# Input projection of a hybrid encoder block: stores issued by ScalarE, modulation sums as float32r halves, transposes of k some steps later

## Chip, cores and metric

The kernel runs on one core of one Trainium2 chip. The metric is the device time of one execution in microseconds (us). Before the change it is 2694.75 us, the median of 3 runs (2694.58 to 2695.16).

## What is computed

One encoder layer over 2048 tokens of width 1024, all in float32 (D = 1024, 8 query heads and 2 key/value heads of 64, pooling width 512, feed-forward width 2816):

```python
mod = silu(c) @ w_ada + b_ada                     # 6 sections of 1024: sh1, sc1, g1, sh2, sc2, g2
h = rmsnorm(x, norm1_g) * (1 + sc1) + sh1
proj = h @ w_in                                   # [q 512 | k 128 | v 128 | pool 512]
q = apply_axial_rope(rmsnorm(q, q_norm_g)); k = apply_axial_rope(rmsnorm(k, k_norm_g))
att = blocked_gqa(q, k, v)                        # softmax over all 2048 keys
pool = pool_mixer(u_pool, w_pool, pool_scale)     # windows 2, 4, 8, 16
x = x + g1 * (concat(att, pool) @ w_out)
h2 = rmsnorm(x, norm2_g) * (1 + sc2) + sh2
x = x + g2 * conv_gated_ffn(h2, w_up, conv_w, conv_b, w_down)
```

## The kernel before

The whole layer is one program in three stages: the input projection (here up to about 380 us), attention with the output projection, and the feed-forward part. The tile framework sets the semaphores and plans the order of each engine's instructions by its own estimate of when they are ready; some instructions are pinned to the order in which they are written. Each engine takes its queue strictly in order, and a transfer waits in the queue of the engine that issues it until its data are there. SP issues nearly all transfers.

Precision is kept by splitting each float32 operand into a part rounded to float32r (`hi`) and the rest (`lo`), and by three float32r matmuls (hi x hi, hi x lo, lo x hi) for one product. A matmul on float32 data that are not split is one of true float32; the trace shows it as more than one instruction.

**Start.** The modulation sections 1 and 0 are needed first. `gen_acc` (L184) loads the eight 128x1024 tiles of a section of w_ada and VectorE adds them up, each scaled by its entries of silu(c), into `acc` (128 partitions x 1024); what is left is a sum over the partitions. `mod_col` (L205) does it with eight float32 matmuls of one column against ones and gives the section as a column per chunk of 128. The small vectors (b_ada, norms, conv weights) come as rows (L142 to L150), are transposed by TensorE and copied to `cols`. w_in is loaded and split in ten pieces (L321).

**Loop over eight blocks of 256 tokens** (L577). Its TensorE work is `gen_u` (pooling channels, 96 matmul steps) and twice `gen_qkv` (24 steps of two matmuls each); after every step the loop advances generators of other work, each at a rate of its own:

- `nxt` is `gen_h` (L268): load x, its mean of squares on ScalarE, scaling, transposes (L290), modulation, split;
- `ropes` is `gen_rope` (L410): norms of q and k and the rotary positions, on VectorE, POOL and ScalarE, a step every 9 (in the last block 4 in the slow stretch);
- `tr_g` is `gen_tr` (L449): transposes of k (`trk`, L456) and q (`tr`, L470), copied to `kst` and `qst` and stored to k_scr and q_scr; a step every 4 (2 in the slow stretch);
- `mix` is `gen_mix` (L514): windows of the pooling mixer on VectorE, its matmuls `pm` (L535), the results `mst`, stored to mix_scr; a step every 4 (2 in the slow stretch);
- `late` (L569), a step every 8: `gen_row(2)`, `gen_col(3)`, `gen_col(4)`, `gen_row(5)`, the other four modulation sections. `gen_row` sums over the partitions with a 128x128 of ones, so that each partition has the whole row, and adds b_ada by a second matmul of one partition (L242, L243, true float32). After section 2 it scales w_out by the gate, splits it, and stores both parts to wo_scr (L262, L263).

In the last block the order is q, k, v first and then the pooling channels, and `early` (L552) computes some of the maxima of attention's first unit.

**To attention.** k, v and q go through device memory (k_scr, v_scr, q_scr). The last 256 keys are loaded by POOL (L653) once their stores have landed; the matmuls `pmx` (L692) of the first unit need them. SP then loads the split w_out (`wo`, L651), the pooling results (`mix`, L810) and x (L839).

Of the kernel before, what the change touches and what calls it, by code (L numbers as in the profile page):

```python
# [14 lines left out]
ALU = mybir.AluOpType  # L15
# [49 lines left out]
def hybrid_block(ctx: ExitStack, tc: tile.TileContext, x, c, w_ada, b_ada, norm1_g, w_in,  # L65
# [12 lines left out]
    def rows(v):  # L78
        return v.rearrange("(a p) -> a p", p=P)
# [45 lines left out]
    with tc.tile_pool(name="p1", bufs=1) as p1, \  # L125
# [16 lines left out]
        SP.dma_start(out=rows_a[8:56], in_=rows(b_ada))  # L142
        SP.dma_start(out=rows_a[56:64], in_=rows(norm1_g))
        SP.dma_start(out=rows_a[64:72], in_=rows(norm2_g))
        SP.dma_start(out=rows_a[72:76], in_=rows(pool_scale))
        SP.dma_start(out=rows_a[76:120], in_=rows(conv_b))
        cw = conv_w.rearrange("w (a p) -> (w a) p", p=P)
        SP.dma_start(out=rows_a[120:124], in_=cw[128:132])
        rows_b = p1.tile([P, P], F32, tag="rows", name="rows_b", bufs=2)
        SP.dma_start(out=rows_b, in_=cw[0:128])  # L150
# [5 lines left out]
        g10 = p1.tile([P, 10, HD], F32, name="g10")  # L156
        qkrow = p1.tile([P, P], F32, tag="rows", name="qkrow", bufs=2)[0:1, :]
        SP.dma_start(out=qkrow[:, 0:64], in_=q_norm_g.unsqueeze(0))
        SP.dma_start(out=qkrow[:, 64:128], in_=k_norm_g.unsqueeze(0))
        gq = ps1.tile([P, 512], F32, tag="tp", name="gq", bufs=2)  # L160
        PE.matmul(gq[:, 0:128], ones[0:1, :], qkrow, start=True, stop=True)
        for h in range(10):
            V.tensor_copy(out=g10[:, h], in_=gq[:, 0:64] if h < 8 else gq[:, 64:128])
# [40 lines left out]

        def mod_col(sec, slot, acc):  # L205
            ps = ps1.tile([P, 512], F32, tag="pu", name=f"mc{sec}", bufs=2)
            for j in range(KD):
                PE.matmul(ps[:, j:j + 1], acc[:, j * P:(j + 1) * P], ones[:, 0:1], start=True, stop=True)
            tc.keep_in_program_order(
                V.tensor_tensor(out=mod_c[:, slot], in0=ps[:, 0:KD],  # L210
                                in1=cols[:, CB + 8 * sec:CB + 8 * sec + 8], op=ALU.add))
# [11 lines left out]
        def gen_col(sec, slot, cn=None):  # L223
            acc = new_acc(sec)
            yield from gen_acc(sec, acc, stage, eng=BG)
            for _ in range(4):
                yield
            mod_col(sec, slot, acc)
            if cn is not None:
                mod_scale(slot, cn)  # L230
            yield

        def gen_row(sec, slot):
            acc = new_acc(sec)
            yield from gen_acc(sec, acc, stage, eng=BG)
            brow = stage()
            SP.dma_start(out=brow[0:1], in_=b_ada[sec * D:(sec + 1) * D].unsqueeze(0))
            for _ in range(4):
                yield
            for n in range(2):  # L240
                ps = ps1.tile([P, 512], F32, tag="pu", name=f"mr{sec}_{n}", bufs=2)
                PE.matmul(ps, ones, acc[:, n * 512:(n + 1) * 512], start=True, stop=False)  # L242
                PE.matmul(ps, ones[0:1, :], brow[0:1, n * 512:(n + 1) * 512], start=False, stop=True)  # L243
                V.tensor_copy(out=acc[:, n * 512:(n + 1) * 512], in_=ps)
                yield
            if slot == 1:
                SP.dma_start(out=g_scr, in_=acc)
                return
            wss = {}
            ks = (4, 5, 6, 7, 0, 1, 2, 3)  # L250
            for i, k in enumerate(ks):
                for k_ in ks[i:i + 2]:
                    if k_ not in wss:
                        wss[k_] = stage()
                        SP.dma_start(out=wss[k_], in_=w_out[k_ * P:(k_ + 1) * P])
                yield
                ws = wss[k]
                BG.tensor_tensor(out=ws, in0=ws, in1=acc, op=ALU.mult)
                wh = p1.tile([P, D], F32R, tag="woh", name=f"woh{k}", bufs=1)
                S.copy(out=wh, in_=ws)  # L260
                BG.tensor_tensor(out=ws, in0=ws, in1=wh.bitcast(F32), op=ALU.subtract)
                SP.dma_start(out=wo_scr[0, k * P:(k + 1) * P], in_=wh.bitcast(F32))  # L262
                SP.dma_start(out=wo_scr[1, k * P:(k + 1) * P], in_=ws)  # L263
                yield

# [115 lines left out]
        def gen_qkv(b, t, chains):  # L381
# [23 lines left out]
            SP.dma_start(out=v_scr[tok:tok + P], in_=vst.bitcast(F32))  # L405
            cs_t = p1.tile([P, 2, HD], F32, tag="rope", name=f"rope{tok}", bufs=2)
            SP.dma_start(out=cs_t, in_=rope[tok:tok + P])
            chains.append((b, tok, raw, cs_t))

        def gen_rope(b, tok, raw, cs_t, res):  # L410
# [3 lines left out]
            V.tensor_tensor(out=raw, in0=raw, in1=g10, op=ALU.mult)  # L414
# [34 lines left out]
        def gen_tr(tok, qhl, khl):  # L449

            for _ in range(4):
                yield
# [9 lines left out]
            SP.dma_start(out=k_scr[:, :, :, tok:tok + P].rearrange("i a p t -> p (i a) t"), in_=kst)  # L462
# [11 lines left out]
            SP.dma_start(out=q_scr[:, :, tok:tok + P].rearrange("h p t -> p h t"), in_=qst)  # L474
# [39 lines left out]
        def gen_mix(b, us):  # L514
# [10 lines left out]
            for i, g in enumerate(groups(b)):  # L525
# [5 lines left out]
                for _ in range(3):  # L531
                    yield
# [8 lines left out]
            i0 = 8 if b == 0 else 0  # L541
            for i in range(2):
                SP.dma_start(out=mix_scr[i, :, :, t0 - 8 + i0:t0 - 8 + nout].rearrange("g p t -> p g t"),
                             in_=mst[i][:, :, i0:nout].bitcast(F32))
# [890 lines left out]
```

## Time and profile before

| | |
|---|---|
| median of 3 runs | 2694.75 us |
| profiled execution, its own time | 2694.41 us |
| span of the profile | 2692.6 us |
| granted clock of TensorE, mean | 0.988 of full speed |
| TensorE, busy share of the span | 96% |
| VectorE, POOL, ScalarE | 72%, 60%, 57% |
| DMA, read and written | 249.42 and 86.63 MB |

How to read the rows further down. Engines are PE (TensorE matmuls), PEld (its weight loads), DVE (VectorE), ACT (ScalarE), POOL (GpSimd) and SP. In a row of stretches stand the start and end in us, the length, and for PE, PEld, DVE, ACT and POOL the busy time with the number of instructions; then the granted clock as a share of full speed (2.4 GHz; 0.50 is 1.2 GHz), the mean busy share of the 16 DMA engines (above 1 where transfers overlap) and the rate in GB/s. A row of waits reads "who waited, at which line, for whom: us in total, times, longest". A row of groups names line, engine, operation, output and inputs, shape and count, then busy time and mean duration in ns, and the idle time of the engine ahead of it with its releaser. Durations of matmuls overlap, since they are pipelined. A row in order of time has the start, the duration and, in brackets, the idle time before and what ended it.

### The profile page before, as it was taken

The page shows a single profiled execution, that of the slowest core. Times are in us where ns is not written, and L with a number is a line of the kernel's source. Part 1 is how long each engine was busy: PE and PEld are TensorE (multiplying, and loading weights), DVE is VectorE, ACT ScalarE, POOL GpSimd, SP SyncE. Part 2 cuts the span into 40 slices and gives each one's busy share as a digit, 9 for nine tenths or more (in the row PEclk, how much of TensorE's full clock was granted, in tenths as well). Part 3 has the DMA queues.
Part 4 walks back from the last instruction along what each step waited for, and adds up shares of the span by engine and source line. Part 5 has one row for each costly group of instructions (what it writes and reads, how often), then busy time and mean ns, then how long its engine had stood idle before and what let it go on. Part 6 is the DMA issues. An engine that isn't in the chain of part 4 may idle for free.

```text
span 2692.6 us, 38997 instructions
## 1 busy us (share of the span) xinstructions
PE 2577.8 (96%) x13439; PEld 2232.5 (83%) x13439; DVE 1926.2 (72%) x3014; ACT 1544.4 (57%) x2848; POOL 1615.7 (60%) x1397
## 2 busy tenths in 40 slices
PE   5899989999999999989899999899999999999999
PEld 5788877777776776767898999699999998999998
DVE  7877678889999999888577776745555557455554
ACT  5565457767778777776654555554343445544442
POOL 1222135656566666664887887586565676777673
PEclk9999989999999999999999999999999999999999
DMA  9685373431222122223544444533332325333332
GB/s 293 233 266 180 100 242 103 149 100 58 71 63 77 58 76 69 78 88 120 172 149 135 148 132 139 195 106 103 105 106 94 95 78 189 114 122 118 110 110 86
DMA packets 318161, 338.61 MB, mean 126 GB/s; under 512 B 24656, under 2 KB 226330, under 8 KB 317962
## 3 DMA queue, kind: packets, MB, share of 16 engines
q1 hardware_dynamic: 316953, 332.31, 39.1%
q0 software_dynamic: 1008, 3.81, 0.5%
q8 instruction: 105, 1.72, 0.3%
q14 instruction: 95, 0.77, 0.1%
HBM read 249.42 MB, written 86.63 MB: 125 GB/s over the span
## 4 chain that ended last, share of the span: by engine, by line
PE 47%; DVE 2%; POOL 1%; ACT 1%; issue 1%; DMA 0%; DVEq 0%; SPq 0%; POOLq 0%; ACTq 0%
PE py L1248 16%; PE px L1159 13%; PE pw L1159 9%; PE pz L1159 8%; PE pl L1377 1%; DVE b L993 0%; POOL wl_s L1035 0%; ACT hb L977 0%; POOL t L1000 0%; DVE y L1253 0%; DMA wr<-in_w_up_dram 0%; POOL t L1007 0%; POOL wl_a L1035 0%; ACT ac L1218 0%; DVE t L993 0%
## 5 line engine op out<-in xcount | busy, mean ns | idle before, releaser
L741 POOL TENSOR_TENSOR acc<-acc,ph 128x512 f32<-128x512 f32 x352 | 463.6, 1317 | 40.7 <-ACT ph L735 15.5
L1035 POOL TENSOR_TENSOR wl_s<-s,wh_s 128x512 fp32r<-128x512 f32 x260 | 349.6, 1346 | 204.7 <-ACT wh_s L1033 202.1
L735 ACT ACTIVATE ph<-S 128x512 fp32r<-128x512 f32 x512 | 306.9, 600 | 130.0 <-PE S L732 114.3
L737 DVE TENSOR_TENSOR pl<-S,ph 128x512 fp32r<-128x512 f32 x512 | 348.0, 683 | 40.0 <-ACT S L736 33.0
L1253 DVE TENSOR_TENSOR y<-py,y 128x512 f32<-128x512 f32 x300 | 205.8, 688 | 222.4 <-PE py L1248 220.7
L694 DVE TENSOR_REDUCE mx<-pmx 128x1 f32<-128x512 f32 x500 | 337.4, 680 | 25.9 <-PE pmx L692 23.9
L1033 ACT CAST wh_s<-s 128x512 fp32r<-128x512 f32 x264 | 163.5, 621 | 313.0 <-PE pw L1159 146.8
L1035 POOL TENSOR_TENSOR wl_a<-wr,wh_a 128x512 fp32r<-128x512 f32 x195 | 266.7, 1374 | 104.7 <-ACT wh_a L1033 104.3
L736 ACT ACTIVATE S<-S 128x512 f32<-128x512 f32 x512 | 306.5, 599 | 0.0
L1248 PE MATMUL py<-wdh,gh 128*128 128x512 f32 x664 | 261.7, 395 | 1.9 <-DVE y L1253 1.7
L1248 PE MATMUL py<-wdh,gl 128*128 128x512 f32 x664 | 262.1, 395 | 0.0
L1248 PE MATMUL py<-wdl,gh 128*128 128x512 f32 x664 | 261.8, 395 | 0.0
L1033 ACT CAST wh_a<-wr 128x512 fp32r<-128x512 f32 x198 | 122.3, 618 | 240.8 <-PE pz L1159 202.4
L1159 PE MATMUL px<-t,wh_s 128*128 128x322 f32 (+1 forms) x1024 | 247.9, 322 | 5.3 <-ACT p1s L1192 3.6
L724 PE MATMUL B<-pl,vt 128*128 128x512 f32 x512 | 210.5, 411 | 5.3 <-DVE pl L737 5.0
L723 PE MATMUL A<-ph,vt 128*128 128x512 f32 x512 | 204.6, 408 | 5.3 <-ACT ph L735 5.3
L692 PE MATMUL pmx<-kA,qa 128*128 128x512 f32 x500 | 203.2, 408 | 3.4 <-DMA kA<-k_scr 2.5
L732 PE MATMUL S<-qb,kB 65*128 65x512 f32 x512 | 202.8, 402 | 1.1 <-ACT qb L702 0.8
L731 PE MATMUL S<-qa,kA 128*128 128x512 f32 x512 | 202.4, 398 | 0.0
L739 POOL TENSOR_TENSOR acc<-ph,ph 128x512 f32<-128x512 f32 x32 | 41.3, 1290 | 255.4 <-ACT ph L735 234.9
L1159 PEld LDWEIGHTS px<-t,wh_s 128*128 128x128 f32 x1024 | 178.3, 189 | 12.3 <-ACT p1s L1192 4.4
L1159 PE MATMUL px<-t,wl_s 128*128 128x322 f32 (+1 forms) x512 | 164.2, 321 | 0.0
(297 smaller groups left out, 6877.9 us busy)
## 6 DMA issues: line engine op xcount, KB each, us to landing
wr<-in_w_up_dram SPq DMA_DIRECT2D x132, 512.0 KB
wdh<-wd_scr SPq DMA_DIRECT2D x88, 256.0 KB
wdl<-wd_scr SPq DMA_DIRECT2D x88, 256.0 KB
stage<-in_w_ada_dram SPq DMA_DIRECT2D x36, 512.0 KB
x_scr<-x SPq DMA_DIRECT2D x48, 256.0 KB
wds<-in_w_down_dram SPq DMA_DIRECT2D x44, 256.0 KB
wd_scr<-wdh SPq DMA_DIRECT2D x44, 256.0 KB
wd_scr<-wdl SPq DMA_DIRECT2D x44, 256.0 KB
```

The lines of the kernel that those rows point to most:

```text
L694: V.tensor_reduce(out=mx[:, qt, j:j + 1], in_=ps, axis=AX.X, op=ALU.max)
L723: PE.matmul(A, vt[:, kt, 192 * a:192 * a + P], ph, start=kt == 0, stop=kt == NKT - 1)
L724: PE.matmul(B, vt[:, kt, 64 + 64 * a:192 + 64 * a], pl, start=kt == 0, stop=False)
L735: S.activation(out=ph, in_=s, func=AF.Exp, scale=0.125)
L736: S.activation(out=s, in_=s, func=AF.Exp, scale=0.125)
L737: V.tensor_tensor(out=pl, in0=s, in1=ph.bitcast(F32), op=ALU.subtract)
L741: G.tensor_tensor(out=acc, in0=acc, in1=ph.bitcast(F32), op=ALU.add)
L1033: S.copy(out=hf, in_=src)
L1035: eng.tensor_tensor(out=lf, in0=src, in1=hf.bitcast(F32), op=ALU.subtract)
L1159: mm = PE.matmul(ps, l_[:, k], r_[:, k, 0:N], start=first and k == 0 and m == 0, stop=k == 3 and m == 2, skip_group_check=not first)
L1248: PE.matmul(ps, l_[:, ts_], r_, start=i == 0, stop=i == 3 * len(js) - 1)
L1253: V.tensor_tensor(out=ys[t][:, ns], in0=ps, in1=ys[t][:, ns], op=ALU.add)
```

## The change

- The nine small loads ahead of the modulation (rows_a, rows_b, qkrow) are issued by POOL in place of SP.
- The weights of the q and k norms are kept once each (`g2`) and broadcast over the heads; the product is two instructions (8 heads, 2 heads) in place of one.
- For the four late sections the accumulated sum is split into two float32r tiles (`halves`: a copy on ScalarE, a subtraction on VectorE), and the sums over partitions are float32r matmuls of both halves; `gen_row` adds b_ada on one partition before the split. Two more turns of `late` stand before the split (in `gen_row` one more behind the bias). The halves take the two buffers of the tag `stage`.
- The stores of v, k, q, the pooling results and w_out are issued by ScalarE. The store of v moves into the first step of `gen_rope`, those of w_out and of the pooling results come one step after their producers. The rotary tables get 4 buffers in place of 2.
- `gen_tr` waits 7 steps in place of 4 before its first transpose, `gen_mix` 5 in place of 3 before a group's matmuls.

```diff
--- before.py
+++ after.py
@@ -139,28 +139,29 @@
...
         G.memset(rows_a, 0.0)
-        SP.dma_start(out=rows_a[8:56], in_=rows(b_ada))
...
+        G.dma_start(out=rows_a[8:56], in_=rows(b_ada))
...
         cw = conv_w.rearrange("w (a p) -> (w a) p", p=P)
-        SP.dma_start(out=rows_a[120:124], in_=cw[128:132])
+        G.dma_start(out=rows_a[120:124], in_=cw[128:132])
         rows_b = p1.tile([P, P], F32, tag="rows", name="rows_b", bufs=2)
-        SP.dma_start(out=rows_b, in_=cw[0:128])
+        G.dma_start(out=rows_b, in_=cw[0:128])
         tp = ps1.tile([P, 512], F32, tag="tp", name="tpc", bufs=2)
...
-        g10 = p1.tile([P, 10, HD], F32, name="g10")
+        g2 = p1.tile([P, 2, HD], F32, name="g2")
+        ones_r = p1.tile([P, P], F32R, name="ones_r")
+        V.tensor_copy(out=ones_r, in_=ones)
         qkrow = p1.tile([P, P], F32, tag="rows", name="qkrow", bufs=2)[0:1, :]
-        SP.dma_start(out=qkrow[:, 0:64], in_=q_norm_g.unsqueeze(0))
-        SP.dma_start(out=qkrow[:, 64:128], in_=k_norm_g.unsqueeze(0))
+        G.dma_start(out=qkrow[:, 0:64], in_=q_norm_g.unsqueeze(0))
+        G.dma_start(out=qkrow[:, 64:128], in_=k_norm_g.unsqueeze(0))
         gq = ps1.tile([P, 512], F32, tag="tp", name="gq", bufs=2)
         PE.matmul(gq[:, 0:128], ones[0:1, :], qkrow, start=True, stop=True)
-        for h in range(10):
-            V.tensor_copy(out=g10[:, h], in_=gq[:, 0:64] if h < 8 else gq[:, 64:128])
+        V.tensor_copy(out=g2.rearrange("p a d -> p (a d)"), in_=gq[:, 0:128])
@@ -202,12 +203,26 @@
...
+        def halves(sec, acc):
+            hl = [p1.tile([P, D], F32R, tag="stage", name=f"acc{i}_{sec}", bufs=2) for i in range(2)]
+            S.copy(out=hl[0], in_=acc)
+            V.tensor_tensor(out=hl[1], in0=acc, in1=hl[0].bitcast(F32), op=ALU.subtract)
+            return hl
+
         def mod_col(sec, slot, acc):
             ps = ps1.tile([P, 512], F32, tag="pu", name=f"mc{sec}", bufs=2)
-            for j in range(KD):
-                PE.matmul(ps[:, j:j + 1], acc[:, j * P:(j + 1) * P], ones[:, 0:1], start=True, stop=True)
+            if isinstance(acc, list):
+                for j in range(KD):
+                    for i, a_ in enumerate(acc):
+                        PE.matmul(ps[:, 2 * j:2 * j + 2], a_[:, j * P:(j + 1) * P], ones_r[:, 0:2],
+                                  start=i == 0, stop=i == 1)
+                sums = ps[:, 0:2 * KD].rearrange("p (k i) -> p k i", i=2)[:, :, 0]
+            else:
+                for j in range(KD):
+                    PE.matmul(ps[:, j:j + 1], acc[:, j * P:(j + 1) * P], ones[:, 0:1], start=True, stop=True)
+                sums = ps[:, 0:KD]
             tc.keep_in_program_order(
-                V.tensor_tensor(out=mod_c[:, slot], in0=ps[:, 0:KD],
+                V.tensor_tensor(out=mod_c[:, slot], in0=sums,
                                 in1=cols[:, CB + 8 * sec:CB + 8 * sec + 8], op=ALU.add))
@@ -223,9 +238,12 @@
...
             yield from gen_acc(sec, acc, stage, eng=BG)
+            for _ in range(2):
+                yield
+            hl = halves(sec, acc)
             for _ in range(4):
                 yield
-            mod_col(sec, slot, acc)
+            mod_col(sec, slot, hl)
             if cn is not None:
@@ -235,12 +253,17 @@
...
             SP.dma_start(out=brow[0:1], in_=b_ada[sec * D:(sec + 1) * D].unsqueeze(0))
+            for _ in range(2):
+                yield
+            V.tensor_tensor(out=acc[0:1], in0=acc[0:1], in1=brow[0:1], op=ALU.add)
+            yield
+            hl = halves(sec, acc)
             for _ in range(4):
...
                 ps = ps1.tile([P, 512], F32, tag="pu", name=f"mr{sec}_{n}", bufs=2)
-                PE.matmul(ps, ones, acc[:, n * 512:(n + 1) * 512], start=True, stop=False)
-                PE.matmul(ps, ones[0:1, :], brow[0:1, n * 512:(n + 1) * 512], start=False, stop=True)
+                for i, a_ in enumerate(hl):
+                    PE.matmul(ps, ones_r, a_[:, n * 512:(n + 1) * 512], start=i == 0, stop=i == 1)
                 V.tensor_copy(out=acc[:, n * 512:(n + 1) * 512], in_=ps)
@@ -259,9 +282,9 @@
...
                 BG.tensor_tensor(out=ws, in0=ws, in1=wh.bitcast(F32), op=ALU.subtract)
-                SP.dma_start(out=wo_scr[0, k * P:(k + 1) * P], in_=wh.bitcast(F32))
-                SP.dma_start(out=wo_scr[1, k * P:(k + 1) * P], in_=ws)
-                yield
+                yield
+                S.dma_start(out=wo_scr[0, k * P:(k + 1) * P], in_=wh.bitcast(F32))
+                S.dma_start(out=wo_scr[1, k * P:(k + 1) * P], in_=ws)
@@ -402,16 +425,18 @@
...
                                 op=ALU.subtract)
-            SP.dma_start(out=v_scr[tok:tok + P], in_=vst.bitcast(F32))
-            cs_t = p1.tile([P, 2, HD], F32, tag="rope", name=f"rope{tok}", bufs=2)
+            cs_t = p1.tile([P, 2, HD], F32, tag="rope", name=f"rope{tok}", bufs=4)
             SP.dma_start(out=cs_t, in_=rope[tok:tok + P])
-            chains.append((b, tok, raw, cs_t))
-
-        def gen_rope(b, tok, raw, cs_t, res):
+            chains.append((b, tok, raw, cs_t, vst))
+
+        def gen_rope(b, tok, raw, cs_t, vst, res):
             E = V if b >= RB else G
...
             S.activation(out=t1, in_=raw, func=AF.Square)
-            V.tensor_tensor(out=raw, in0=raw, in1=g10, op=ALU.mult)
+            for i, (h0_, h1_) in enumerate(((0, 8), (8, 10))):
+                V.tensor_tensor(out=raw[:, h0_:h1_], in0=raw[:, h0_:h1_],
+                                in1=g2[:, i].unsqueeze(1).broadcast_to([P, h1_ - h0_, HD]), op=ALU.mult)
+            S.dma_start(out=v_scr[tok:tok + P], in_=vst.bitcast(F32))
             yield
@@ -448,7 +473,7 @@
...
-            for _ in range(4):
+            for _ in range(7):
                 yield
@@ -459,7 +484,7 @@
...
             S.copy(out=kst, in_=tr.bitcast(F32))
-            SP.dma_start(out=k_scr[:, :, :, tok:tok + P].rearrange("i a p t -> p (i a) t"), in_=kst)
+            S.dma_start(out=k_scr[:, :, :, tok:tok + P].rearrange("i a p t -> p (i a) t"), in_=kst)
             if tok >= T - BT:
@@ -471,7 +496,7 @@
...
                 S.copy(out=qst[:, hb * 4:hb * 4 + 4], in_=tr.bitcast(F32))
-            SP.dma_start(out=q_scr[:, :, tok:tok + P].rearrange("h p t -> p h t"), in_=qst)
+            S.dma_start(out=q_scr[:, :, tok:tok + P].rearrange("h p t -> p h t"), in_=qst)
@@ -528,7 +553,7 @@
...
                 ph, pl = res[i]
-                for _ in range(3):
+                for _ in range(5):
                     yield
@@ -539,8 +564,9 @@
...
             i0 = 8 if b == 0 else 0
+            yield
             for i in range(2):
-                SP.dma_start(out=mix_scr[i, :, :, t0 - 8 + i0:t0 - 8 + nout].rearrange("g p t -> p g t"),
+                S.dma_start(out=mix_scr[i, :, :, t0 - 8 + i0:t0 - 8 + nout].rearrange("g p t -> p g t"),
                              in_=mst[i][:, :, i0:nout].bitcast(F32))
```

## Rows read from the trace of the kernel before

**Rows 1.** The page, part 1: busy us of each engine over the span.

```profile
PE 2577.8 (96%) x13439; PEld 2232.5 (83%) x13439; DVE 1926.2 (72%) x3014; ACT 1544.4 (57%) x2848; POOL 1615.7 (60%) x1397
```

**Rows 2.** Stretches of time: the engines from PE to POOL, clock, DMA share, GB/s.

```profile
39.00:380.00 341.00, 310.50 (x2006) 284.13 (x2004) 259.22 (x508) 193.79 (x438) 74.59 (x104) 0.96 0.62 197
87.40:90.70 3.30, 3.30 (x18) 3.30 (x17) 3.30 (x5) 0.00 (x0) 0.00 (x0) 0.50 0.46 159
238.40:244.90 6.50, 6.50 (x34) 6.50 (x33) 4.27 (x9) 2.22 (x6) 0.00 (x0) 0.54 0.20 81
375.00:394.50 19.50, 14.64 (x33) 8.42 (x34) 11.54 (x23) 6.21 (x11) 5.46 (x7) 0.50 1.04 371
```

**Rows 3.** TensorE's waits, 45 to 425 us: us in total, times, longest.

```profile
PE mr L242 <- DVE macc L200: 6.4, 2, 4.8
PE trk L456 <- ACT khl L437: 5.6, 3, 3.0
PE tp L290 <- ACT xt L278: 3.8, 3, 1.8
PE pm L535 <- DVE mst L539: 3.2, 2, 2.7
...
PE pm L535 <- ACT ph L508: 2.3, 3, 1.0
```

**Rows 4.** Groups by shape, 45 to 425 us: busy us, mean ns, idle before.

```profile
L242 PE MATMUL mr<-macc,ones 128*128 128x512 f32 x8 | 6.8, 972 | 6.4 <-DVE macc L200 6.4
...
L243 PE MATMUL mr<-stage,ones 1*128 1x512 f32 x8 | 5.2, 759 | 0.0
...
L565 PE MATMUL pme<-k_early,q_early 128*128 128x512 f32 x12 | 5.0, 413 | 0.0
```

**Rows 5.** SP in order of time: start us, us, what.

```profile
70.89 3.12 SPq L190 DMA_DIRECT2D stage<-in_w_ada_dram  x2
```

**Rows 6.** Issues of two stores by SP (ns), waits of SP and ScalarE.

```profile
L405 SPq DMA_DIRECT2D v_scr<-vst x16: 319/330/1831, 74.1 to 355.3; - x16
...
L543 SPq DMA_DIRECT2D mix_scr<-mst x16: 359/408/2697, 109.8 to 379.5; - x16
...
SPq L405 <- DVE vst L403: 20.6, 12, 3.9
...
ACT junk L276 <- DMA xt<-in_x_dram: 13.3, 5, 5.9
```

**Rows 7.** Groups by shape, 45 to 425 us, VectorE and ScalarE.

```profile
L414 DVE TENSOR_TENSOR raw<-raw,g 128x640 f32<-128x640 f32 x16 | 13.1, 819 | 2.2 <-ACT t L413 2.1
...
L444 DVE TENSOR_TENSOR qhl<-raw,qhl 128x512 fp32r<-128x512 f32 x16 | 11.0, 684 | 1.3 <-ACT qhl L443 1.2
...
L261 DVE TENSOR_TENSOR stage<-stage,woh 128x1024 f32<-128x1024 f32 x8 | 9.8, 1219 | 1.7 <-ACT woh L260 1.7
...
L260 ACT CAST woh<-stage 128x1024 fp32r<-128x1024 f32 x8 | 8.4, 1052 | 4.9 <-DVE stage L258 4.9
...
L438 DVE TENSOR_TENSOR khl<-raw,khl 128x128 fp32r<-128x128 f32 x16 | 4.6, 286 | 4.6 <-ACT khl L437 4.6
```

**Rows 8.** The start: two stretches; SP and VectorE in order of time.

```profile
0.00:10.00 10.00, 0.24 (x1) 0.18 (x1) 7.12 (x6) 3.04 (x4) 3.61 (x79) 1.00 0.74 269
10.00:20.00 10.00, 1.89 (x7) 1.26 (x7) 7.25 (x16) 1.01 (x2) 0.00 (x0) 1.00 0.86 294
...
9.11 0.35 SPq L150 DMA_DIRECT2D rows_b<-in_conv_w_dram  x1
...
21.99 0.75 DVE L198 TENSOR_SCALAR macc<-big_h_lo,cact 128x1024 f32<-128x1024 f32 x1 [2.52 <-DMA big_h_lo<-in_w_ada_dram]
```

**Rows 9.** The end of the projection: POOL, SP and TensorE in order of time.

```profile
376.65 0.57 POOL L653 DMA_DIRECT2D kA<-k_scr  x1 [2.90 <-DMA k_scr<-kst]
...
380.02 2.03 SPq L651 DMA_DIRECT2D wo<-wo_scr  x2
...
382.19 1.22 PE L692 MATMUL pmx<-kA,qa 128*128 128x512 f32 x2 [2.46 <-DMA kA<-k_scr]
```

More of the change, by code (lines that the diff above doesn't have):

```diff
@@ L141, in hybrid_block @@
         G.memset(rows_a, 0.0)
-        SP.dma_start(out=rows_a[8:56], in_=rows(b_ada))
[L143 to L146, printed above, removed]
+        G.dma_start(out=rows_a[8:56], in_=rows(b_ada))
+        G.dma_start(out=rows_a[56:64], in_=rows(norm1_g))
+        G.dma_start(out=rows_a[64:72], in_=rows(norm2_g))
+        G.dma_start(out=rows_a[72:76], in_=rows(pool_scale))
+        G.dma_start(out=rows_a[76:120], in_=rows(conv_b))
         cw = conv_w.rearrange("w (a p) -> (w a) p", p=P)
-        SP.dma_start(out=rows_a[120:124], in_=cw[128:132])
+        G.dma_start(out=rows_a[120:124], in_=cw[128:132])
         rows_b = p1.tile([P, P], F32, tag="rows", name="rows_b", bufs=2)
-        SP.dma_start(out=rows_b, in_=cw[0:128])
+        G.dma_start(out=rows_b, in_=cw[0:128])
         tp = ps1.tile([P, 512], F32, tag="tp", name="tpc", bufs=2)
```

## The prediction

> **What bounds the kernel now.** I read the page's busy shares first: TensorE is busy in 96% of the span, no other engine above 72% [rows 1], so time is lost only where TensorE idles, runs at its low clock or does dear work. The change touches the input projection alone, so the table by stretches comes next. From 39 to 380 us TensorE is busy 310.50 of 341.00 us at a mean granted clock of 0.96 [rows 2]: 30.5 us of idle, and 0.04 x 341 = 13.6 us given to the 1.2 GHz level. ScalarE, which is to get new work, is busy 193.79 of the 341 (57%), VectorE 259.22 (76%) [rows 2]. The list of waits names who held TensorE up [rows 3]; the groups by shape price what goes [rows 4].
>
> **Row sums.** gen_row for the sections 2 and 5 adds up 128 partitions with true float32 matmuls: 8 instructions of L242 (6.8 us) and 8 of L243 (5.2 us), 12.0 us in all [rows 4]. Now there are two rows x two column halves x two operand halves = 8 float32r matmuls, 128x512. The nearest row is L565, the same shape and type: 0.41 us on average, ends overlapping [rows 4]. Its neighbours start closer than that, so 8 of them lie between 8 x 0.2 = 1.6 us (half of the row's mean, an estimate) and 3.3 us. I take 2.0: **10.0 us saved** (8.7 to 10.4), all on TensorE.
>
> **Clock behind the row sums.** Right after the first sum, from 87.4 to 90.7 us, the granted clock is 0.50, and after the second, from 238.4 to 244.9 us, 0.54 [rows 2], with TensorE busy throughout. What came before was in both cases a wait and then the float32 sums. At full clock the two stretches would take 1.65 and 3.5 us: 1.65 + 3.0 = **4.6 us saved** if neither remains, 0 if the clock falls all the same.
>
> **The wait ahead of them.** TensorE waited 6.4 us for VectorE's accumulation, 4.8 of them at once, ahead of the first sum [rows 3]. That accumulation was late because SP issued its last two weight tiles only from 70.89 us on, the two issues stretched over 3.12 us [rows 5]. The new order puts two or three more turns of `late` and a split between accumulation and matmul; a turn is 8 steps of the main loop. I take **5.0 us** (0 to 6.4). Queued behind the new sums is only other projection work, which runs in the meantime.
>
> **Transposes of k and pooling matmuls.** TensorE waited 5.6 us for khl on ScalarE [rows 3]; three further yields (12 main-loop steps normally, 6 in the slow stretches) put other matmuls there. I take **4.0 us** (0 to 5.6). The pooling matmul waited 3.2 us for mst and 2.3 us for ph [rows 3]; two more yields help where other work is left, not at the very end of the projection. I take **2.5 us** (0 to 5.5).
>
> **Stores leave SP.** 80 stores (v, k, q, mix, w_out) go to ScalarE. On SP each took about 0.33 us (v, median) to 0.41 us (mix, median), with single ones of 1.8 and 2.7 us under load [rows 6]: about 80 x 0.38 = 30 us that SP is rid of. More matters that SP stood in a store until its producer was done, for v alone 20.6 us behind VectorE [rows 6], with loads queued behind. ScalarE waited 13.3 us for x, and TensorE then 3.8 us for the scaled x [rows 3, 6]. I take half of the latter, **1.9 us** (0 to 3.8). The Trainium skill, page "DMA: Bandwidth & Descriptors", section "Issuing engines are not separate DMA queues", says that issuing from several engines saves only the sequencer's time to issue, as all share the same DMA engines. By it the term is 0 and the earlier loads are no earlier; the row of 20.6 us speaks against it here, as a blocked queue is no matter of bandwidth. What that mechanism would give is the second rival.
>
> **What ScalarE pays.** The trace has no DMA issued by ScalarE. Nearest are SP's rows: 30 us, on a queue busy 57%, so it rises to some 66%. If nothing of it shows on TensorE the price is 0; if every issue delays TensorE, 30 us. Between: TensorE's waits for ScalarE in the list (khl, xt, ph) are 11.7 us against 193.79 us of ScalarE's work, 0.06 per us, and 30 x 0.06 = 1.8. Since stores also wait for VectorE's halves (v, mix, w_out) with evictions of PSUM queued behind, I take **5 us**, nearer the low end. The k and q stores follow their own copy on ScalarE and add no foreign wait.
>
> **VectorE.** Added: four subtractions of 1024 columns (1.22 us each), two bias additions of the same width on one partition, and 16 times 0.68 + 0.29 in place of 0.82 us for the norm weights [rows 7]: 4.9 + 2.4 + 2.4 = 9.7 us on a queue that is busy 76%. ScalarE gets four copies at 1.05 us [rows 7]. What hides this is the slack of the late sums: the second stretch of low clock behind them ended at 244.9 us [rows 2], some 135 us before the projection does. I take **1 us** (0 to 9.7). Column sums: 32 instructions are replaced by 32 matmuls of two columns; I take 0.
>
> **Start.** Nine small loads leave SP for POOL. SP issued rows_b only at 9.11 us, ahead of w_ada tiles, while the DMA engines were used at 0.74 and 0.86 in the first two tens of us [rows 8]: 2.6 + 1.4 = 4.0 us of room. VectorE's accumulation later stood 2.52 us for such a tile [rows 8]. The gain is at most 4.0 us; if POOL brings the small rows later, VectorE's copy of them stands in the chain, and up to that 2.52 us could be lost. I take **3.0 us saved**.
>
> **End.** In the last block the three yields count: 6 main-loop steps. 2006 matmuls over 341 us [rows 2] are 0.17 us each, with two or so per step: some 2 us by which the last k comes later. Behind it hang its store, the load of kA, which POOL issued at 376.65 us after 2.90 us of waiting for that store, and the first matmul at 382.19 us, which waited 2.46 us [rows 9]. I take **2 us lost** (0 to 4).
>
> **Sum.** Saved 10.0 + 4.6 + 5.0 + 4.0 + 2.5 + 1.9 + 3.0 = 31.0; lost 5 + 1 + 2 = 8; net 23. The profiled execution took 2694.41 us (span 2692.6 and 1.8 around it), 0.3 below the median of the runs, 2694.75. So 2694.75 - 23 = 2671.7 us.
>
> **Rivals.**
> 1. *ScalarE's queue becomes the brake (slower).* Place: copies out of PSUM (u, raw, kst, qst, mst) behind a store that waits or whose issue is stretched. For it: single issues of 1.8 and 2.7 us, and VectorE's lag of 20.6 us over 12 v stores [rows 6]. Against: ScalarE has 43% idle, and a store comes one turn after its producer. It decides once a store costs TensorE more than (31 - 3)/80 = 0.35 us; at 0.5 us it is 40 us lost: 2694.7 - 31 + 3 + 40 = 2707 us. Chance 0.12.
> 2. *SP's freedom buys nothing.* Loads land when they did; then the 1.9, the 5.0 and the first clock stretch's 1.65 us stay: 2671.7 + 8.5 = 2680 us. For it: DMA share of 0.62 over the projection [rows 2]. Against: rows 5. Chance 0.17.
> 3. *Given back at the change of stage.* Freed of stores, SP could issue the two loads of wo (2 MB each), at 380.02 us until now [rows 9], ahead of the small kA load on which attention starts. 4.2 MB at the 371 GB/s of that stretch [rows 2] is 11 us: 2671.7 + 11 = 2683 us. Against: their memory has to come free first. Chance 0.13.
> 4. *It doesn't do what it says.* The planner moves the waits elsewhere, the clock falls as before, and ScalarE takes the sum's 10 us: 2693 us. Chance 0.08.
>
> **How the numbers follow.** Forecast 0.50, with a range of its own of 2661 to 2680. What a measurement here tells from no change is about 0.2%, 5.4 us. Faster: 0.50 + 0.17 + 0.13 = 0.80; same 0.08; slower 0.12. The range for 8 in 10: down to 2658, where all savings stand at their better ends (10.4 + 4.6 + 6.4 + 5.6 + 5.5 + 3.8 + 4.0 = 40.3), ScalarE costs nothing and VectorE and the end keep their 3 us, and up to 2694, which takes in rivals 2 to 4 and leaves most of the first out.
>
> **What would show it.** In the changed profile: matmuls of the row sums near 0.4 us and no wait for macc ahead; the clock at 1.00 behind them; waits for khl and for xt under 2 us each; ScalarE's copies without waits for VectorE ahead of stores; VectorE's wait of 2.52 us for a w_ada tile gone; the first kA matmul some 20 us before 382. It is wrong if TensorE's idle time in the projection stays near 30 us with ScalarE as releaser, or if the attention starts no earlier.

## The result and the profile after

The changed kernel takes 2716.84 us (median of 4 runs, 2716.54 to 2718.55) against 2694.66 us (4 runs, 2692.78 to 2695.16) for the kernel before on the same chip: ratio 1.0083, 95% interval 1.007 to 1.0096. It is 22 us slower where 23 us faster was forecast. The profiled execution took 2716.9 us, its span is 2715.1 us, 22.5 more than before. Line numbers have moved: `pmx` is L718, the kA loads L679, the wo loads L677, the w_out load L278 and its stores L286 and L287.

The page, part 1, hardly differs from [rows 1]. TensorE is busy 95% of a longer span, where it was 96%:

```profile
PE 2574.0 (95%) x13431; PEld 2240.3 (83%) x13431; DVE 1930.6 (71%) x3028; ACT 1551.6 (57%) x2852; POOL 1631.6 (60%) x1406
```

The stretches say where. Columns as in [rows 2]; the first row answers to its first one:

```profile
39.00:380.00 341.00, 294.77 (x1944) 281.61 (x1944) 257.73 (x511) 192.45 (x425) 78.43 (x95) 0.94 0.58 186
...
83.00:92.00 9.00, 9.00 (x70) 8.70 (x68) 5.63 (x9) 4.39 (x10) 2.44 (x3) 1.00 0.47 148
246.00:260.00 14.00, 13.60 (x85) 12.91 (x84) 13.99 (x31) 11.91 (x28) 5.46 (x5) 1.00 0.51 163
...
100.00:160.00 60.00, 39.09 (x202) 36.72 (x203) 34.44 (x55) 22.12 (x46) 4.71 (x7) 0.77 0.75 260
...
390.00:404.00 14.00, 0.17 (x1) 0.17 (x2) 0.06 (x1) 0.00 (x0) 0.71 (x2) 0.50 1.03 332
```

Behind both row sums (at 84 and 247 us) the clock is 1.00, where it was 0.50 and 0.54. But from 100 to 160 us TensorE is busy 39.1 of 60 us at a mean clock of 0.77, and from 390 to 404 us it stands while the DMA engines are full. The loss is in these two places. The kernel before had this row in the first place:

```profile
100.00:160.00 60.00, 54.59 (x352) 51.97 (x352) 46.72 (x87) 34.24 (x77) 14.94 (x13) 0.97 0.83 276
```

TensorE's waits, 45 to 425 us, against [rows 3], and the row sums by shape against [rows 4]:

```profile
PE pmx L718 <- DMA kA<-k_scr: 14.6, 1, 14.6
PE pu L397 <- DVE mst L564: 9.8, 6, 3.0
PE pb L414 <- ACT raw L419: 7.9, 3, 5.4
PE trk L481 <- DVE vst L426: 6.9, 1, 6.9
...
L266 PE MATMUL mr<-acc,ones_r 128*128 128x512 f32 x8 | 2.9, 417 | 0.4 <-ACT acc L208 0.4
```

The waits that the forecast wanted gone are gone or small: the sums' (6.4 to 0.4 us), and the sums themselves take 2.9 us where 12.0 stood. Others have come: for mst, vst and raw, all halves and PSUM copies of VectorE and ScalarE, and 14.6 us for kA.

ScalarE (and its DMA queue, ACTq) in order of time, inside the first place:

```profile
121.01 1.04 ACT L283 CAST woh<-stage 128x1024 fp32r<-128x1024 f32 x1 [3.88 <-DVE stage L281]
121.96 0.56 ACT L318 ACTIVATE hf<-tp,mod_c 128x256 f32<-128x256 f32 x1
122.08 0.33 ACTq L286 DMA_DIRECT2D wo_scr<-woh  x1
123.34 0.33 ACTq L287 DMA_DIRECT2D wo_scr<-stage  x1
123.71 0.62 ACT L320 CAST h_hi<-hf 128x512 fp32r<-128x512 f32 x1 [1.19 <-DVE stage L284]
...
141.14 2.32 ACTq L569 DMA_DIRECT2D mix_scr<-mst  x2
143.56 1.30 ACTq L286 DMA_DIRECT2D wo_scr<-woh  x1
144.95 1.20 ACTq L287 DMA_DIRECT2D wo_scr<-stage  x1
146.19 0.48 ACT L419 COPY raw<-pa 128x384 f32<-128x384 f32 x1 [4.48 <-DMA q_scr<-qst]
```

A turn of the w_out loop can hold ScalarE at three points: before the copy `woh`, for VectorE's product; when that copy wants the one `woh` buffer that a store still reads; and before the second store, for VectorE's subtraction (some 1.2 us, with h_hi or raw queued behind). ScalarE's waits from 95 to 160 us have the first two; in the kernel before the first came to 4.9 us (3 times) and the second was not there:

```profile
ACT woh L283 <- DVE stage L281: 11.7, 4, 3.9
...
ACT woh L283 <- DMA wo_scr<-woh: 6.6, 2, 3.5
```

At 141 us four issues stand in a row for 4.8 us, and raw, for which TensorE then waits, behind them. (The bracket of raw names the landing of a q store; the row itself starts 0.04 us after the last of the four issues ends.)

The loop itself has not become slower. Its eight copies by line and tile (durations in ns, first and last start), the kernel before and then the changed one:

```profile
L260 ACT CAST woh<-stage x8: 1028/1052/1063, 91.6 to 145.4; 128x1024 fp32r<-128x1024 f32 x8
```

```profile
L283 ACT CAST woh<-stage x8: 1044/1046/1059, 92.4 to 140.7; 128x1024 fp32r<-128x1024 f32 x8
```

That is 53.8 / 7 = 7.7 us a turn before and 6.9 now. What has changed is who keeps step with it: ScalarE executes 46 instructions from 100 to 160 us in place of 77. SP is not freer for it. The waits of its DMA queue (SPq) from 95 to 160 us, the kernel before and then the changed one:

```profile
SPq L255 <- DMA wo_scr<-stage: 9.3, 5, 2.6
SPq L262 <- ACT woh L260: 8.8, 3, 4.2
SPq L262 <- ACT ph L508: 7.2, 2, 6.3
SPq L262 <- ACT u L377: 3.6, 1, 3.6
SPq L263 <- DVE stage L261: 2.9, 3, 1.6
SPq L263 <- DVE pl L509: 2.7, 2, 1.5
```

```profile
SPq L278 <- DMA wo_scr<-stage: 33.8, 6, 8.5
```

A w_out load needs a tile whose store has landed. Before, SP stood 9.3 us in the loads (L255) and 25.2 us in the stores of the loop, 34.5 together; now it stands 33.8 us in the loads alone.

The second place, in order of time (compare [rows 9]):

```profile
384.33 0.94 SPq L677 DMA_DIRECT2D wo<-wo_scr  x2
385.32 7.36 SPq L836 DMA_DIRECT2D mix<-mix_scr  x2
...
384.61 0.57 POOL L679 DMA_DIRECT2D kB<-k_scr  x1 [12.39 <-PE tr L495]
...
387.38 0.59 POOL L679 DMA_DIRECT2D kA<-k_scr  x1
...
388.96 9.40 ACTq L569 DMA_DIRECT2D mix_scr<-mst  x2
...
403.83 1.22 PE L718 MATMUL pmx<-kA,qa 128*128 128x512 f32 x2 [14.61 <-DMA kA<-k_scr]
```

And the kA load of 128 KB in the list of DMA issues, with the median us to landing last, the kernel before and then the changed one:

```profile
kA<-k_scr POOLq DMA_DIRECT2D x1, 128.0 KB, 5.5
```

```profile
kA<-k_scr POOLq DMA_DIRECT2D x1, 128.0 KB, 16.4
```

Before, SP issued the last mix stores, then the wo loads, at 380.02 us, behind the kA load at 376.65 us. Now wo goes out 3.05 us ahead of kA, and kA lands after 16.4 us in place of 5.5. SP stood ready for it; until 384.33 us it waited only for the memory that wo goes to:

```profile
SPq L677 <- PE tr L495: 11.6, 1, 11.6
```

The first `pmx` starts at 403.83 us, 21.6 us later than before; that is nearly the whole difference of the spans (from there to the end 2311.3 us, before 2310.4).

### The profile page after: what moved, and what is told of

The parts are those of the page before. It is cut to its first block, busy times and chain, and to the rows that moved or that the text cites. A ratio compares the mean times of both kernels' runs of the same rounds, so it can differ in the third digit from the quotient of the medians.

```text
span 2715.1 us, 38997 instructions
## 1 busy us (share of the span) xinstructions
PE 2574.0 (95%) x13431; PEld 2240.3 (83%) x13431; DVE 1930.6 (71%) x3028; ACT 1551.6 (57%) x2852; POOL 1631.6 (60%) x1406
## 3 DMA queue, kind: packets, MB, share of 16 engines
q1 hardware_dynamic: 278494, 300.72, 35.2%
q10 hardware_dynamic: 38144, 31.46, 3.5%
## 4 chain that ended last, share of the span: by engine, by line
PE 47%; DVE 2%; ACT 1%; POOL 1%; issue 1%; DVEq 0%; POOLq 0%; ACTq 0%
PE py L1274 16%; PE px L1185 13%; PE pw L1185 9%; PE pz L1185 8%; PE pl L1403 1%; DVE b L1019 0%; ACT hb L1003 0%; POOL wl_s L1061 0%; POOL t L1026 0%; POOL t L1033 0%; DVE y L1279 0%; ACT ac L1244 0%; DVE t L1019 0%; DVE ac L1247 0%; ACT t L1018 0%
## 5 line engine op out<-in xcount | busy, mean ns | idle before, releaser
L718 PE MATMUL pmx<-kA,qa 128*128 128x512 f32 x500 | 203.2, 408 | 15.5 <-DMA kA<-k_scr 14.6
```

## The experiments

All in 5 rounds against the kernel before (its median was between 2694.15 and 2695.08 us in all of them). The start of the first `pmx` and the span are of the one profiled execution, which need not be a typical one: that of e17 took 8 us more than the median of its runs, those of e12 and e15 nearly 5 us less.

| run | median us | ratio, 95% interval | first pmx, us | span, us |
|---|---|---|---|---|
| before | | | 382.2 | 2692.6 |
| changed | 2716.84 | 1.0083 [1.007, 1.0096] | 403.8 | 2715.1 |
| e1_stores | 2736.49 | 1.0154 [1.0138, 1.017] | 425.5 | 2735.8 |
| e2_sums | 2698.0 | 1.0008 [0.9996, 1.002] | 382.6 | 2694.6 |
| e3_steps | 2702.6 | 1.003 [1.0021, 1.0038] | 387.9 | 2700.0 |
| e4_start | 2688.24 | 0.9978 [0.9969, 0.9987] | 372.8 | 2685.8 |
| e5_wout_sp | 2704.18 | 1.0037 [1.0025, 1.005] | 389.5 | 2701.0 |
| e6_mix_sp | 2710.22 | 1.0059 [1.0046, 1.0072] | 395.5 | 2705.7 |
| e7_kv_sp | 2705.32 | 1.004 [1.0027, 1.0052] | 389.1 | 2701.8 |
| e8_wout_only | 2720.52 | 1.0096 [1.008, 1.0111] | 406.8 | 2720.2 |
| e9_wout_pool | 2712.54 | 1.0066 [1.0053, 1.0078] | 399.7 | 2710.7 |
| e10_both | 2694.34 | 1.0002 [0.999, 1.0014] | 380.0 | 2691.0 |
| e11_both_steps | 2695.26 | 1.0004 [0.9995, 1.0013] | 377.6 | 2693.3 |
| e12_no_sums | 2698.67 | 1.0014 [1.0005, 1.0023] | 376.4 | 2692.3 |
| e13_no_act_stores | 2694.15 | 0.9998 [0.9989, 1.0007] | 376.3 | 2692.4 |
| e14_vkq_act | 2686.92 | 0.9968 [0.9958, 0.9979] | 377.3 | 2688.5 |
| e15_sp_steps | 2688.54 | 0.9978 [0.9967, 0.9988] | 370.2 | 2682.0 |
| e16_two_undone | 2698.04 | 1.0011 [1.0002, 1.0021] | 384.3 | 2696.4 |
| e17_two_undone_no_sums | 2704.21 | 1.0036 [1.0024, 1.0049] | 396.2 | 2710.7 |
| e18_wout_sp_late | 2703.85 | 1.0033 [1.0021, 1.0045] | 396.7 | 2705.2 |

**One part alone, on the kernel before.** e1 moves all 80 stores:

```diff
-                SP.dma_start(out=wo_scr[0, k * P:(k + 1) * P], in_=wh.bitcast(F32))
+                S.dma_start(out=wo_scr[0, k * P:(k + 1) * P], in_=wh.bitcast(F32))
 (and the stores of v, k, q and mix; g2 and 4 rotary buffers, so that it fits)
```

> The kernel before with only the 80 stores issued by ScalarE (with their new places, 4 buffers for the rotary tables, and the norm weights kept once, without which the tiles don't fit). Theory A (ScalarE's queue is the brake: copies out of PSUM stand behind stores that wait for VectorE or for a buffer): this part alone is slower, 2704 to 2720 us, with TensorE idle near 100 to 160 us and ScalarE waiting between its copies. Theory B (the loss comes from the later transposes of k, which delay the last stores and so POOL's loads until they share the DMA engines with the loads of the split w_out): 2690 to 2697 us, and the load of the last keys lands in under 8 us.

41 us slower, beyond the expected band, with both losses in it: TensorE's clock from 100 to 160 us, and the wait for kA.

```profile
100.00:160.00 60.00, 36.25 (x192) 34.48 (x192) 29.45 (x42) 20.35 (x41) 2.75 (x5) 0.69 0.78 269
...
PE pmx L694 <- DMA kA<-k_scr: 13.4, 1, 13.4
```

k's transposes wait 4 yields here as before, so the late kA is not their doing. e2 has the sums alone (`halves`, float32r matmuls, their turns, g2):

```diff
+            hl = halves(sec, acc)
-                PE.matmul(ps, ones, acc[:, n * 512:(n + 1) * 512], start=True, stop=False)
+                    PE.matmul(ps, ones_r, a_[:, n * 512:(n + 1) * 512], start=i == 0, stop=i == 1)
```

> The kernel before with only the late modulation sums as float32r halves with their extra turns (and the norm weights kept once). Both theories: faster, 2680 to 2688 us, 10 us from the sums themselves and up to 4.6 from the clock behind them. If the sums did not pay: 2694 us or more, with the granted clock low behind them all the same.

No gain, where both theories expected 2680 to 2688 us. The cheaper matmuls are there, and the clock is 1.00 behind the first sum (87.6 to 92 us) and 0.87 behind the second (260.5 to 268 us). There are other waits, too: the wait for macc has become one for the copy of the half on ScalarE, the one for xt has grown (3.8 us in [rows 3]), and the one for raw has come up.

```profile
PE pb L414 <- ACT raw L419: 6.4, 2, 4.8
PE tp L313 <- ACT xt L301: 5.3, 2, 2.8
...
PE mr L266 <- ACT acc L208: 4.2, 1, 4.2
```

e3 has the later steps alone:

```diff
-            for _ in range(4):
+            for _ in range(7):
 (gen_tr; in gen_mix 3 becomes 5)
```

> The kernel before with only the later transposes (7 steps in place of 4) and the later pooling matmuls (5 in place of 3). Theory A: 2688 to 2696 us, some waits for khl and mst go. Theory B: slower, 2700 to 2710 us, all of the loss between the last projection matmul and the first pmx matmul, with the load of kA landing in over 10 us.

7.5 us slower, which is theory B's band: kA is issued 1.9 us later than before and lands after 9.4 us in place of 5.5 (theory B wanted over 10), and `pmx` starts 5.7 us later. So the later steps alone can delay attention. But a late kB does not make the long wait of the changed kernel: POOL waits there as long, SP still has the mix stores ahead of wo, and `pmx` waits 3.45 us for kA and not 14.6:

```profile
375.75 0.58 POOL L653 DMA_DIRECT2D kB<-k_scr  x1 [11.62 <-PE pu L374]
378.54 0.57 POOL L653 DMA_DIRECT2D kA<-k_scr  x1
...
383.75 3.04 SPq L543 DMA_DIRECT2D mix_scr<-mst  x2
386.89 3.12 SPq L651 DMA_DIRECT2D wo<-wo_scr  x2
```

e4 has the start alone (small loads by POOL, g2):

```diff
-        SP.dma_start(out=rows_b, in_=cw[0:128])
+        G.dma_start(out=rows_b, in_=cw[0:128])
```

> The kernel before with only the nine small loads issued by POOL and the norm weights kept once. Both theories: 2689 to 2694 us; the first pu matmul comes 2 to 5 us earlier than at 39.4 us.

6.8 us faster, just past the expected band; the first `pu` matmul comes 3.2 us earlier (36.2 us), as expected. From 10 to 20 us the DMA share is 1.03, where it was 0.86 [rows 8], and `pmx` starts 9.4 us earlier. The norm weights (g2) changed with the loads here and were not tried alone.

**One part undone, in the changed kernel.** e5, the w_out stores back on SP:

```diff
-                yield
-                S.dma_start(out=wo_scr[0, k * P:(k + 1) * P], in_=wh.bitcast(F32))
+                SP.dma_start(out=wo_scr[0, k * P:(k + 1) * P], in_=wh.bitcast(F32))
 (likewise wo_scr[1]; the yield follows)
```

> The changed kernel with only the sixteen w_out stores back on SP. Theory A (two losses: the compute queue of ScalarE is held by w_out stores that wait for VectorE's subtraction and for their one buffer, about 10 us at 100 to 160 us; and about 12 us at the change of stage, because SP, rid of stores, issues the wo loads ahead of the kA load): 2702 to 2709 us, TensorE's clock at 100 to 160 us back to 0.9 or more, the wait of the first attention matmul for kA still above 10 us. Rival C (the loss in the projection comes from the v, k, q and mix stores, of which there are 64, not from these 16): 2714 to 2720 us and the low clock stays.

As theory A has it: 12.7 us back, TensorE busy again from 100 to 160 us, the wait for kA still 13.7 us.

```profile
100.00:160.00 60.00, 53.70 (x354) 51.73 (x352) 48.61 (x96) 39.49 (x87) 17.33 (x18) 0.94 0.87 299
```

e6, the mix stores back on SP:

```diff
-            yield
             for i in range(2):
-                S.dma_start(out=mix_scr[i, ...
+                SP.dma_start(out=mix_scr[i, ...
```

> The changed kernel with only the sixteen mix stores back on SP. Theory A: SP has to stand in the last mix stores again, so the wo loads go out behind the kA load; the first attention matmul waits for kA some 3 us and no longer 14.6: 2702 to 2708 us, with the loss at 100 to 160 us left as it is. Rival D (the wo loads are late or early by their memory alone, whatever SP did before): wo still ahead of kA, wait above 10 us, 2713 to 2720 us.

The mechanism is as expected (SP stands in mix stores until 391.8 us, wo follows, `pmx` waits 4.0 us for kA); the time, 2710.22 us, is above the band, a gain of 6.6 us. e7 leaves all stores where the change put them and only turns the order of the loads:

```diff
-        load_kv(0, ((T - BT, T),))
+        load_kv(0, ((T - BT, T),), True)
 (True: kA, kB, vt of the last block are issued by SP, ahead of wo)
```

> The changed kernel, where the last pieces of k and v for the attention (kA, kB, vt of the last block) are loaded by SP, in its queue ahead of the wo loads, and no longer by POOL behind a load that waits for memory. All stores stay on ScalarE. Theory A: order alone decides, the wait for kA falls from 14.6 to 3 to 6 us, 2703 to 2709 us. Rival D2 (the transfers are slow for another reason, the stores of the last k, q and mix on the same DMA engines): kA still lands 12 to 16 us after its issue although the wo loads are behind it, 2713 to 2718 us.

11.5 us back: the order decides. `pmx` waits 1.43 us. e7 also turns these loads from POOL's queue to SP's; e6, where POOL issues them and wo comes behind, has nearly the same short wait (4.0 us), so it is not the queue.

```profile
384.57 0.32 SPq L677 DMA_DIRECT2D kA<-k_scr  x1
384.98 0.36 SPq L677 DMA_DIRECT2D kB<-k_scr  x1
385.98 1.73 SPq L677 DMA_DIRECT2D wo<-wo_scr  x2
...
389.13 1.19 PE L718 MATMUL pmx<-kA,qa 128*128 128x512 f32 x2 [1.43 <-DMA kA<-k_scr]
```

e8 moves only the 16 w_out stores in the kernel before (the first diff above, with the yield ahead):

> The kernel before with only the sixteen w_out stores moved to ScalarE (one turn later, as in the change). Theory A: TensorE's clock falls at 100 to 160 us as it did with all 80 stores, 2701 to 2712 us, first attention matmul's wait for kA near 3 us since the mix stores stay on SP. Rival C: 2692 to 2697 us, no low clock there.

25.8 us slower, more than expected; the clock from 100 to 160 us is 0.77, TensorE busy 37.4 us, and the wait for kA 3.1 us. The loss from 100 to 160 us is these 16 stores'.

**Which queue.** In e9 POOL issues the w_out stores, in e18 SP does, but one step late as in the change:

```diff
-                S.dma_start(out=wo_scr[0, k * P:(k + 1) * P], in_=wh.bitcast(F32))
+                G.dma_start(out=wo_scr[0, k * P:(k + 1) * P], in_=wh.bitcast(F32))
 (e18: SP.dma_start; likewise wo_scr[1])
```

> The changed kernel with the sixteen w_out stores issued by POOL, at the same place in the program as ScalarE's. Theory A (what costs is that ScalarE stands in the store with PSUM copies queued behind it): TensorE's clock at 100 to 160 us back above 0.9, 2701 to 2710 us, since POOL has little that TensorE waits for. Rival E (the stores come later than on SP and with them the next w_out load, since the tile is free only when its store has landed; the loop's own pace is the loss, whoever issues): the clock there stays under 0.85 and the time at 2713 to 2720 us.

> The changed kernel with the w_out stores issued by SP again, but still one step later than in the kernel before. If the engine is what counts (ScalarE stands in the stores, and the stores stand behind ScalarE's other work): SP's waits of w_out loads for landed stores fall to some 13 us, as with the stores back at their old place, and the time is 2702 to 2707 us. If the later step is what counts (the two tiles come back a step later, and the next load with them): these waits stay near 30 us and the time is 2711 to 2718 us.

e18 gave back 13.0 us, all that e5 did, and SP's waits of w_out loads for landed stores fell from 33.8 to 10.3 us: the later step costs nothing, the engine does. With POOL the first place is nearly mended, as theory A has it:

```profile
100.00:160.00 60.00, 51.38 (x322) 48.83 (x321) 42.42 (x80) 35.01 (x76) 16.45 (x26) 0.91 0.89 303
```

ScalarE gets its 76 instructions done. But only 4.3 us came back, between the two bands. POOL now stands in the loop's stores, and SP still waits 31.9 us in the w_out loads, which is rival E's mechanism. From 160 to 240 us TensorE is busy 66.7 us, where the changed kernel has 74.8; e18 has no more there (65.9 us) and is 8.7 us faster, so that stretch does not set the two apart. What e9 loses against e18 was not settled.

**Both repairs, and what is left.** e10 joins e5 and e7; e11 takes the later steps out as well; e12 also the sums.

```diff
 e10: the diffs of e5 and e7        e11: and 7 -> 4, 5 -> 3 yields        e12: and halves out, float32 sums
```

> The changed kernel with both repairs: w_out stores back on SP, and the last block's k and v loads on SP ahead of the wo loads. Theory A: the two losses are separate and add up, 2717 - 12.7 - 11.5 = 2693 us, 2689 to 2697. Rival F (one of them hides the other, as the planner lays everything out anew): 2700 to 2705 us.

> As the kernel with both repairs, and k's transposes and the pooling matmuls again after 4 and 3 yields as in the kernel before. Theory G (later transposes push out the last k and cost 5 to 8 us, as they did alone): 2683 to 2689 us. Rival H (with the other parts in place the later transposes cost nothing or help, as forecast): 2691 to 2698 us.

> As the last one, with the modulation sums done in float32 as before: what is left of the change is the start, the norm weights, and the v, k, q and mix stores on ScalarE. Theory I (the cheaper sums save nothing of the time, as when they were done alone, since VectorE's subtractions and ScalarE's copies take the place): within 3 us of the run with sums. Rival J (they save what the shorter matmuls and the full clock behind them promise, and their price alone was one of place): 10 to 18 us slower than the run with sums.

e10 came out on 2694.34, as the sum of the two (2716.84 - 12.7 - 11.5 = 2692.6) has it: the two repairs add up and bring back the time of the kernel before. That leaves nothing of what the start and the sums should gain. e11 says that the later steps cost nothing here (rival H), e12 that the sums are worth 3.4 us, at the edge of theory I. e13 to e17 looked for the start's 6.8 us, which e10 should still have:

```diff
 e13: changed kernel, all 80 stores on SP, 4 and 3 yields    e14: as e13, v, k, q stores on ScalarE
 e15: as e13, 7 and 5 yields                                 e16: as e14, 7 and 5 yields    e17: as e16, float32 sums
```

> Start, norm weights and the cheaper sums kept, all 80 stores on SP and k's transposes and pooling matmuls after 4 and 3 yields as before. Theory K (the remaining 64 stores on ScalarE, and the handover that they disturb, take the missing 10 us): 2681 to 2688 us. Rival L (start and sums don't add up, because VectorE's and ScalarE's added work for the sums eats the lead): 2690 to 2696 us.

> As the run without stores on ScalarE, but with the 48 v, k and q stores on ScalarE; mix and w_out stores stay on SP, kA is loaded by POOL as before. Theory K1 (k and v stores cost by holding ScalarE's copies): 4 to 10 us slower than that run. Rival K2 (only the mix and w_out stores, which wait for VectorE or set the order of the loads, cost; v, k and q stores are free): within 2.5 us of it.

> As the run without stores on ScalarE, with k's transposes after 7 and pooling matmuls after 5 yields. Theory G (the later steps cost some 7 us where the mix stores are on SP, since the last kB waits for them and the stores come later): 5 to 9 us slower than that run. Rival H (free, as in the run with both repairs): within 2.5 us of it.

> The changed kernel with two of its parts undone: w_out and mix stores on SP; v, k and q stores on ScalarE, sums, start and later steps as in the change. Theory A (these two groups are the loss, the rest of the change gains): 2681 to 2688 us, first attention matmul at 368 to 376 us in the profile. Rival M (the other stores cost as well, the plan alone decides): 2692 to 2700 us.

> As the run with two groups of stores undone, with the modulation sums in float32 as before. Theory I (sums worth nothing to 3 us): within 3.5 us of that run. Rival J (worth their 10 us of matmul and the clock behind): 8 us or more slower than it.

With 4 and 3 steps, e13 came out as rival L has it and e14 is 7.2 us faster than e13 (K1 wanted it slower, K2 within 2.5 us): there the 48 stores of v, k and q cost nothing on ScalarE. With 7 and 5 steps, which the change has, it is the other way round: e16 differs from e15 in these 48 stores alone (with the place of v's store and the buffers of the rotary tables that go with it) and is 9.5 us slower, and TensorE is busy 9.2 us less from 100 to 240 us (first e15, then e16):

```profile
100.00:240.00 140.00, 129.87 (x880) 123.00 (x879) 116.67 (x219) 88.22 (x194) 33.29 (x42) 0.98 0.84 264
```

```profile
100.00:240.00 140.00, 120.70 (x807) 115.33 (x806) 108.35 (x205) 85.25 (x185) 41.10 (x41) 0.94 0.78 254
```

Theory A's forecast for e16 missed by 10 us, and rival M's band holds it. No single wait carries these 9.5 us, so their cause stays open. The runs also give the whole price of the stores in the change: from e15, without a store on ScalarE, it is 9.5 us to e16 (v, k, q), 6.1 to e5 (mix as well) and 12.7 to the changed kernel (w_out as well), 28.3 us in all.

The later steps gain 5.6 us from e13 to e15 (neither theory G nor rival H), lose 11.1 from e14 to e16, lose 7.5 alone and nothing between e11 and e10: they have no price of their own, and with them neither have the v, k and q stores. The sums are worth 6.2 us in e16 against e17, between its two bands. Single small edits thus differ by 5 to 10 us with what stands beside them; that the planner lays the projection out anew each time is the likely reason, and no run tests it. Why e11 to e13, whose `pmx` starts 4.6 to 5.9 us earlier than before, end no earlier stays open; in e11 and e12 a later `pmx` waits 3.8 us for qa, issued behind wo, which is a part of it.

The best three, e14, e4 and e15, beat both kernels (ratios in the table).

## Why the prediction was wrong

The step that failed is **What ScalarE pays**, put at 5 us lost. It priced 80 issues by their length and held that "a store comes one turn after its producer". The length was about right (0.34 us for v, 0.37 for k and q, median, in the changed trace). But w_out is a loop over load, product, copy, subtraction and store through one `woh` and two `stage` tiles, some 7 us a turn. ScalarE, issuing its stores, went at the loop's pace, and with it its PSUM copies, which TensorE needs. 16 of the 80 stores cost 25.8 us alone and 12.7 in the change. In place of 5 us, with 1.9 saved on SP, all 80 cost 28.3 us: 12.7 for w_out, 6.1 for mix, which is the change of stage below, and 9.5 for v, k and q, whose place was not found and which gained 7.2 us beside the old steps. The first rival named the place and the direction, with a price spread over all stores.

**Stores leave SP** (1.9 us saved) bought nothing in the loop, where SP stands as long as before (34.5 and 33.8 us), as the second rival had it, and had its sign turned at the change of stage. The third rival described it: SP freed of the mix stores issues wo ahead of kA. Its estimate was 11 us; e7 gives 11.5, e6 6.6. Its objection, "their memory has to come free first", did not hold: the memory came free at 384.33 us and SP was there. The Trainium skill, page "DMA: Bandwidth & Descriptors", section "Issuing engines are not separate DMA queues", says that issuing from several engines saves only the issue time. That much agrees: with two queues in place of one the DMA engines moved 260 GB/s from 100 to 160 us, before 276. What decides here is which load a queue gets to first: 16.4 us in place of 5.5 for kA. Rivals one and three came together; the forecast took them as alternatives of 0.12 and 0.13.

**Row sums, clock and wait** (10.0, 4.6 and 5.0 us saved) all came as described: 9.1 us less matmul time, clock 1.00 behind, the wait at 0.4 us. The time did not: nothing alone (e2), 3.4 and 6.2 us in two pairs. What the runs show is that other waits took the place (acc, xt and raw in e2). That TensorE there goes at the pace of ScalarE and VectorE, which got the copies and subtractions, fits this and was not tested by itself. Adding three savings of TensorE's as if it were bound by itself was wrong in a stretch where it idles 30 us: all of the change but the stores was to gain 26 us, and e15, which has just that, gains 5.7. So the miss of 45 us is some 25 of stores and 20 of savings that did not come.

**Transposes of k, pooling matmuls and End** (6.5 saved, 2 lost): the waits for khl went from 5.6 to 1.6 us, but `trk` now waits 6.9 us for vst, and the time has no steady sign. **The start** (3.0 saved) was right in sign and too small: 6.8 us alone (e4). In the changed kernel `mc` shows 3.2 of it (29.53 in place of 32.76 us). **VectorE** (1 us) can't be told apart from the sums.

Of the signs that the forecast named, six came true: the sums, the wait for macc, the clock, khl, xt (0.5 us) and, nearly, VectorE's first wait for a w_ada tile (0.80 us in place of 2.52). ScalarE's copies without waits for VectorE did not, nor the early `pmx`. The two it named as fatal did too: TensorE's idle time from 39 to 380 us grew from 30.5 to 46.2 us, with VectorE as releaser nearly as much as ScalarE, and attention started later.

## What to carry to other kernels

Before moving a DMA to a compute engine's queue, see what loop it stands in: ScalarE, issuing this loop's stores, went at the loop's pace, and here they cost least on SP. When a queue is relieved, look at what stands next in it and whether that will overtake a small transfer on which the next stage starts; set that order by hand. A wait that vanishes from the list is a gain only where nothing else is due at the same place, and effects below some 10 us need the whole change measured, not its parts.

## What the runs showed of the hardware

The stores issued by ScalarE appear as a DMA queue of their own (q10, 31.46 MB in the changed kernel's page, beside q1 with 300.72). An issue mostly takes ScalarE's queue 0.33 to 0.37 us (medians of the v, k, q and w_out stores), like SP's, and 0.53 to 0.65 us on POOL (loads of k and q); with 4 MB of wo under way two mix stores took 9.40 us. A 128 KB load behind those 4 MB took 16.4 us, three times its 5.5, although it was issued by another engine.
